# A hybrid encoder layer: fixed instruction orders from the decay terms to the merge, one step of each chain per weight piece

## The chip, the cores and the metric

One Trainium2 chip, of which the kernel uses 1 core. The metric is the device time of one execution in microseconds (us), as the median of several runs; lower is better. An interval is a 95% one.

## The reference

One layer over 272 positions (16 learned meta tokens and 256 inputs) of width 2048, in float32. One projection `u @ w_in` feeds everything; branch A is a bidirectional mLSTM with 4 heads of 256, branch B a differential attention with 8 heads. The change touches branch A's core and B's queries and keys:

```python
u = rmsnorm(h, norm1_g[layer])
proj = u @ w_in[layer]
m_qk, m_v, m_o, m_gates, d_q, d_k, d_v, g_m, g_d = jnp.split(proj, split_at, axis=-1)
...
qk = jax.nn.silu(dwconv_centred(m_qk, conv_w))
q, k = jnp.split(qk, 2, axis=-1)
...
# one direction, per chunk of the scan
dmat = jnp.where(lower, b[..., :, None] - b[..., None, :] + li[..., None, :], -jnp.inf)
s = jnp.einsum('bhtd,bhsd->bhts', q, k) * jnp.exp(dmat - m_t[..., None])
den = jnp.sum(s, axis=-1) + a_t * jnp.einsum('bhd,bhtd->bht', n, q)
h = num / jnp.maximum(jnp.abs(den), jnp.exp(-m_t))[..., None]
...
# both directions
hs = (h_fwd + h_bwd)[:, :, pad:]
hn = (hs - mu) * lax.rsqrt(var + EPS)
...
q = rope_partial(q, cos, sin)
k = rope_partial(k, cos, sin)
```

The kernel writes the scan as whole 258-column maps: per head one table of decays (`FB`) times the scores, in both directions, without chunks.

## The kernel before

**Weights.** All products run as fp32r pairs: an operand is split into `hi`, its rounded copy, and `lo`, the rest, and a product is three matmuls. The weights come in pieces of 512 KB (`pieces`, from the DMA queue on SP), each split by ACT (`hi` cast, line 157) and DVE (`lo` subtract, line 115) into one of four buffers. `weights()` hands out a piece and prepares the one three ahead. A block of `gemm` makes 256 output columns from four pieces, 24 matmuls to a piece, in two of three PSUM tiles `acc`; after its last piece `evac` copies both halves out, so the second half of the next block waits for the first copy of this one.

**Stages.** After an opening that computes Q's first block and the 16 gate columns, `weave(front, back)` interleaves a front, which is a generator of small steps, with blocks of weights: one front step, then one piece. The fronts are `decay_terms` (gates to decay rows `rows` and columns `aT`, lines 479 to 538) over the rest of Q and all K; `heads1` (lines 655 to 667: per head the decay table, scores, their product, and the sums `den`) over V; `heads2` (lines 726 to 747: reciprocal, spread, merge of both directions, output product, norm) over DQ. DK and DV follow with `run`, without a front.

**Where work waits.** Apart from the opening, the order in which an engine takes its instructions is made by a scheduler from the dependences and its own estimates of time; each engine then works strictly in that order. `in_order()` replaces this for what is written inside it: each instruction is tied behind the one written before it on its engine. The opening uses it already. `later` is a list of functions that `gemm` calls (`flush()`) after the next piece's matmuls.

**POOL.** For each head POOL broadcasts a row of `rows` over 128 partitions (line 606), masks six parts of it (line 609), and later adds four parts of the weighed scores (line 164). PSUM has besides `acc` one tile `one` and two tiles `two`; `den` holds one of the latter through `heads1`.

Of the kernel before, what the change touches and what calls it, by code (L numbers as in the profile page):

```python
# [12 lines left out]
AF = mybir.ActivationFunctionType  # L13
# [51 lines left out]
def hybrid_layer(ctx, tc, x, meta, norm1_g, w_in, conv_w, gate_bias, mnorm_g, lq1, lk1, lq2, lk2,  # L65
# [259 lines left out]

    def rsqrt(r, ss, n, work, bias=eps):

        a, t = work
        activation(r, ss, AF.Ln, bias=bias, scale=1.0 / n)
        activation(r, r, AF.Exp, scale=-0.5)  # L330
        V.tensor_scalar(out=a, in0=ss, scalar1=1.0 / n, scalar2=bias, op0=ALU.mult, op1=ALU.add)
        V.scalar_tensor_tensor(out=t, in0=r, scalar=-0.5, in1=r, op0=ALU.mult, op1=ALU.mult)
        mul(t, t, a)
        V.scalar_tensor_tensor(out=r, in0=t, scalar=1.5, in1=r, op0=ALU.add, op1=ALU.mult)
# [113 lines left out]
    def conv_silu(dst, f, r, nt):  # L448
        hi, lo = pair(nt)
        dst.append((hi, lo))  # L450

        def evac(ci, a):
            j = f + ci
            u, c = r1(nt), r1(nt)
            mul(u, a, r)
            S.activation(c, u, AF.Copy, scale=cw(1, j))
            V.scalar_tensor_tensor(out=c[:, 1:nt], in0=u[:, 0:nt - 1], scalar=cw(0, j), in1=c[:, 1:nt],
                                   op0=ALU.mult, op1=ALU.add)
            V.scalar_tensor_tensor(out=c[:, 0:nt - 1], in0=u[:, 1:nt], scalar=cw(2, j), in1=c[:, 0:nt - 1],  # L459
                                   op0=ALU.mult, op1=ALU.add)  # L460
            activation(c, c, AF.Silu)
            split(hi[:, ci, :], lo[:, ci, :], c)
        return evac

    put = conv_silu(qs, 0, rQ, NT)
# [11 lines left out]
    rows = rbp.tile([P, WN], F32, tag="rb", name="rows")  # L477

    def decay_terms():

        pli, plf = two(), two()
        for d in range(2):
            PE.matmul(pli[:, d, :L], sel[0:32, d * P:(d + 1) * P], gsb[0:32], start=True, stop=True)
            PE.matmul(plf[:, d, :L], sel[0:32, (2 + d) * P:(3 + d) * P], gsb[0:32], start=True, stop=True)
        li, lf, e, y, w = (unit([2, L]) for _ in range(5))
        S.copy(lf, plf[:, :, :L])
        S.copy(li, pli[:, :, :L])

        S.activation(e, lf, AF.Abs)
        activation(e, e, AF.Exp, scale=-1.0)  # L490
# [53 lines left out]
        for b in range(1, 4):  # L544
            yield from gemm(w_in, 16, Q0 + 256 * b, 256, us, T0, NT, conv_silu(qs, 2 * b, rQ, NT))

    weave(decay_terms(), chain(queries(), keys()))


    def values(c0, centred):  # L550

        v0 = [vsm.tile([P, 1024], F32R, tag="vsm", name="v0") for _ in range(2)]
        for t in v0:
            G.memset(t.bitcast(F32), 0.0)
        vs = []

        def put(b):
            v = pair(256)
            vs.append(([v0[0][:, 256 * b:256 * b + 256], v[0][:, 0, :], v[0][:, 1, :]],
                       [v0[1][:, 256 * b:256 * b + 256], v[1][:, 0, :], v[1][:, 1, :]]))  # L560
            vT = []

            def turn():
                pv = two()
                for ci in range(2):
                    for s in range(3):
                        s0 = ST[s][0]
                        PE.transpose(pv[:, ci, P * s:P * (s + 1)], vT[ci][:, s0:s0 + P], ident)  # L568
                pvs = pv[:, :, 0:384].rearrange("p c (s x) -> p s c x", s=3)
                if centred:  # L570

                    mu = sm(3)
                    V.tensor_reduce(out=mu, in_=pvs, axis=AX.XY, op=ALU.add)
                    V.tensor_scalar(out=mu, in0=mu, scalar1=-1.0 / 256, scalar2=None, op0=ALU.mult)
                for s in range(3):
                    n = ST[s][1]
                    ps = pvs[0:n, s]
                    hi, lo = (vs[b][i][s][0:n].rearrange("p (c x) -> p c x", c=2) for i in range(2))
                    if centred:
                        S.activation(hi, ps, AF.Identity, bias=mu[0:n, s:s + 1], scale=1.0)  # L580
                        V.scalar_tensor_tensor(out=lo, in0=ps, scalar=mu[0:n, s:s + 1], in1=hi.bitcast(F32),
                                               op0=ALU.add, op1=ALU.subtract)
                    else:
                        split(hi, lo, ps)

            def evac(ci, a):
                t = r1(L)
# [12 lines left out]
    W, den = [], two()  # L600
    PARTS_W = [(F0c, 0, 0, 258), (F1c, 1, 2, 256), (F2c, 2, 130, 128)], [(B2c, 2, 0, 258), (B1c, 1, 0, 130), (B0c, 0, 0, 2)]

    def decays(h):
# [11 lines left out]
        mask(FB[0:16, B0c:B0c + 2], 2, -T0, 1)  # L615
        mask(FB[:, B1c + 2:B1c + 130], P, 0, 1)
        mask(FB[:, B2c + 130:B2c + 258], P, 0, 1)
        for d, parts in enumerate(PARTS_W):
            for at, s, _, n in parts:
                ap = FB[:, at:at + n]  # L620
                activation(ap, ap, AF.Exp, bias=aT[:, d, s, h:h + 1], scale=1.0)

    def scores(h):
        FB = W[h]
        ps, p0 = two(), one()
        sc = [p0[:, 0:NT], ps[:, 0, 0:NT], ps[:, 1, 0:NT]]
        for s, (s0, n) in enumerate(ST):

            product(sc[s], [([t[:, c, s0:s0 + P] for t in ks[h]], [t[:, c, :] for t in qs[h]]) for c in range(2)])
        for parts in PARTS_W:  # L630
            for at, s, q, n in parts:
                r = ST[s][1]
# [8 lines left out]
        add(r[:, 0:130], FB[:, B2c:B2c + 130], FB[:, B1c:B1c + 130], G)  # L641
        add(f[0:16], f[0:16], FB[0:16, F0c:F0c + NT], G)
        add(r[0:16, 0:2], r[0:16, 0:2], FB[0:16, B0c:B0c + 2], G)
        hi, lo = t2([2, NT], F32R), t2([2, NT], F32R)
        split(hi, lo, fs)
        return hi, lo
# [5 lines left out]

    en = unit([2, NT])

    def heads1():
        activation(en, m[:, :, T0:L], AF.Exp, scale=-1.0)
        decays(0)
        yield
        for h in range(4):
            if h < 3:  # L660
                decays(h + 1)
            hl = scores(h)
            yield
            yield
            yield
            sums(h, hl)
            yield

    vm, gen = values(V0, True)
    weave(heads1(), gen)  # L670


    hn = []
# [14 lines left out]
    def merged(h, rc):  # L688
# [7 lines left out]
        add(FB[:, F1c:F1c + P], FB[:, F1c:F1c + P], FB[:, B1c + 2:B1c + 130])  # L696
        V.tensor_copy(FB[:, F1c - 2:F1c], FB[:, B1c:B1c + 2])
        add(FB[:, B2c + 130:B2c + 258], FB[:, B2c + 130:B2c + 258], FB[:, F2c:F2c + P])
        hl = rbs.tile([P, 2, WN], F32R, tag="w", name="hl")
        hi, lo = hl[:, 0, :], hl[:, 1, :]  # L700
        split(hi[:, 0:774], lo[:, 0:774], FB[:, 0:774])
# [2 lines left out]
    def outputs(h, hl):  # L704
        num = two()
        for c in range(2):
            product(num[:, c, 0:NT], [([vm[h][i][s][:, P * c:P * (c + 1)] for i in range(2)],
                                       [t[:, 258 * s:258 * s + 258] for t in hl]) for s in range(3)])
        sq, hi, lo = t2([2, NT]), t2([2, NT], F32R), t2([2, NT], F32R)
# [3 lines left out]
        return num, hi, lo  # L713

    def normed(h, num, hi, lo):
# [3 lines left out]
        rsqrt(r, var, 256, (r1(), r1()))  # L719
        u = unit([2, NT])  # L720
        hn.append(u)
        for c in range(2):
# [1 line left out]
                                   op0=ALU.mult, op1=ALU.mult)  # L724

    def heads2():
        rec = unit([2, NT])
        S.activation(rec, den[:, :, 0:NT], AF.Abs)
        V.tensor_tensor(out=rec, in0=rec, in1=en, op=ALU.max)
        V.reciprocal(rec, rec)  # L730
        rhl = pair(NT)
        split(*rhl, rec)
        yield
        hl = merged(0, spread(0, rhl))
        yield
        yield
        for h in range(4):
            if h < 3:
                rc = spread(h + 1, rhl)
            o = outputs(h, hl)  # L740
            yield
            if h < 3:
                hl = merged(h + 1, rc)
            normed(h, *o)
            yield
            yield
            yield


    shuffle = [i + 8 if i < 8 else i - 8 if i < 16 else i for i in range(32)]  # L750
# [2 lines left out]
    def roped(dst, c0, t0, nt):  # L753
        def put(b):
            u = unit([2, nt])
            hi, lo = pair(nt)
            dst.append((hi, lo))

            def evac(ci, a):
                S.copy(u[:, ci, :], a)  # L760
                if ci == 1:
                    table = lambda i: rope[:, i:i + 1, t0:t0 + nt].to_broadcast([P, 2, nt])
                    sw = unit([2, nt])
                    V.stream_shuffle(sw, u, shuffle)
                    mul(sw, sw, table(1), G)
                    mul(u, u, table(0))
                    add(u, u, sw)
                    split(hi, lo, u)
            return evac

        for b in range(4):
            yield from gemm(w_in, 16, c0 + 256 * b, 256, us, t0, nt, put(b))

    weave(heads2(), roped(dq, DQ0, T0, NT))
    run(roped(dk, DK0, 0, L))
    vd, gen = values(DV0, False)
    run(gen)

# [359 lines left out]
```

## Time and profile before

| | us |
|---|---|
| median of 3 runs (1567.14 to 1570.07) | 1569.33 |
| the profiled execution | 1567.37 |
| its span | 1565.5 |
| PE busy | 1542.6 (99%) |
| DVE busy | 1028.6 (66%) |
| ACT busy | 763.7 (49%) |
| POOL busy | 81.0 (5%) |

PE runs the matmuls, DVE and ACT the elementwise work, POOL is the slow fourth engine, SP issues DMAs. The profile's list of waits gives for each engine what ended its idle times; the timeline gives single instructions with the idle time ahead of them in brackets; the table of windows gives busy time and PE's granted clock (1.00 is full speed) in chosen stretches. Times are from the start of the span.

### The profile page before, as it was taken

The page shows a single profiled execution, that of the slowest core. Times are in us where ns is not written, and L with a number is a line of the kernel's source. Part 1 is how long each engine was busy: PE and PEld are TensorE (multiplying, and loading weights), DVE is VectorE, ACT ScalarE, POOL GpSimd, SP SyncE. Part 2 cuts the span into 40 slices and gives each one's busy share as a digit, 9 for nine tenths or more (in the row PEclk, how much of TensorE's full clock was granted, in tenths as well). Part 3 has the DMA queues.
Part 4 walks back from the last instruction along what each step waited for, and adds up shares of the span by engine and source line. Part 5 has one row for each costly group of instructions (what it writes and reads, how often), then busy time and mean ns, then how long its engine had stood idle before and what let it go on. Part 6 is the DMA issues. An engine that isn't in the chain of part 4 may idle for free.

```text
span 1565.5 us, 28927 instructions
## 1 busy us (share of the span) xinstructions
PE 1542.6 (99%) x11825; PEld 1491.2 (95%) x11825; DVE 1028.6 (66%) x1617; ACT 763.7 (49%) x1147; POOL 81.0 (5%) x120
## 2 busy tenths in 40 slices
PE   8899989999999999999999999999999999999997
PEld 8899989999999999999999999999888999999887
DVE  6786688758886545665666676666444676766554
ACT  5656445444655433554555444444333444545443
POOL 1130113100000000000110000000000000000000
PEclk9999999999999999999999999999999999999999
DMA  8365425654356655555555556555555556655552
GB/s 261 110 202 161 148 83 166 189 166 132 122 175 202 185 179 188 181 180 185 193 169 181 187 185 187 181 183 180 198 190 188 187 177 188 185 181 185 184 195 95
DMA packets 255386, 274.53 MB, mean 175 GB/s; under 512 B 11492, under 2 KB 233317, under 8 KB 255237
## 3 DMA queue, kind: packets, MB, share of 16 engines
q1 hardware_dynamic: 251378, 268.61, 54.1%
q10 hardware_dynamic: 3875, 4.07, 0.8%
q8 instruction: 93, 1.52, 0.4%
q14 instruction: 40, 0.33, 0.1%
HBM read 270.55 MB, written 2.10 MB: 174 GB/s over the span
## 4 chain that ended last, share of the span: by engine, by line
PE 95%; DVE 2%; ACT 1%; issue 1%; POOL 0%; DMA 0%; SPq 0%; DVEq 0%; POOLq 0%; ACTq 0%
PE acc L172 90%; PE two L172 2%; DVE lo L115 1%; PE two L846 1%; PE one L172 0%; PE one L858 0%; PE two L568 0%; POOL t L712 0%; ACT hi L157 0%; DMA r<-in_norm_g_dram 0%; PE two L977 0%; PE two L965 0%; DVE u L730 0%; DVE u L115 0%; POOL t L164 0%
## 5 line engine op out<-in xcount | busy, mean ns | idle before, releaser
L172 PE MATMUL acc<-u,hi 128*128 128x258 f32 (+1 forms) x6592 | 1201.8, 285 | 4.8 <-DVE r L161 4.8
L172 PEld LDWEIGHTS acc<-u,hi 128*128 128x128 f32 x6592 | 1019.0, 190 | 7.1 <-DVE r L161 5.1
L172 PE MATMUL acc<-u,lo 128*128 128x258 f32 (+1 forms) x3296 | 925.3, 284 | 0.8 <-DVE lo L115 0.8
L115 DVE TENSOR_TENSOR lo<-raw,hi 128x1024 fp32r<-128x1024 f32 (+1 forms) x500 | 616.8, 1234 | 422.1 <-ACT hi L157 420.4
L157 ACT CAST hi<-raw 128x1024 fp32r<-128x1024 f32 (+1 forms) x500 | 523.7, 1048 | 648.1 <-PE acc L172 501.5
L172 PEld LDWEIGHTS acc<-u,lo 128*128 128x128 f32 x3296 | 622.3, 190 | 1.9 <-DVE lo L115 1.2
L172 PE MATMUL acc<-hi,u 128*128 128x512 f32 (+1 forms) x704 | 209.6, 381 | 0.0
L172 PEld LDWEIGHTS acc<-hi,u 128*128 128x128 f32 x704 | 130.7, 190 | 26.3
L172 PE MATMUL acc<-lo,u 128*128 128x512 f32 (+1 forms) x352 | 134.9, 383 | 0.0
L172 PEld LDWEIGHTS acc<-lo,u 128*128 128x128 f32 x352 | 66.2, 188 | 13.6
L161 DVE TENSOR_TENSOR r<-acc,r 128x258 f32<-128x258 f32 x88 | 37.3, 424 | 12.2 <-PE acc L172 12.2
L115 DVE TENSOR_TENSOR u<-r,u 128x256 fp32r<-128x256 f32 (+2 forms) x93 | 37.7, 435 | 4.9 <-ACT u L157 4.4
L1025 ACT ACTIVATE r<-r,fcT 128x256 f32<-128x256 f32 x88 | 39.8, 500 | 0.0
L157 ACT CAST u<-r 128x256 fp32r<-128x256 f32 (+2 forms) x93 | 34.4, 404 | 9.7 <-DVE r L161 7.0
L1026 DVE SCALAR_TENSOR_TENSOR r<-r,fcT,r 128x256 f32<-128x256 f32 x88 | 38.5, 479 | 0.0
L1027 DVE SCALAR_TENSOR_TENSOR r<-r,fcT,r 128x255 f32<-128x255 f32 x88 | 38.4, 478 | 0.0
L151 ACT ACTIVATE r<-r 128x256 f32<-128x256 f32 (+2 forms) x77 | 29.5, 412 | 3.5 <-DVE r L459 3.1
L161 DVE TENSOR_TENSOR r<-r,r 128x256 f32<-128x256 f32 (+1 forms) x57 | 22.1, 420 | 0.1
L161 DVE TENSOR_TENSOR r<-acc,u 128x258 f32<-128x258 f32 x32 | 13.5, 422 | 12.9 <-PE acc L172 12.9
L164 DVE TENSOR_TENSOR u<-acc,u 128x512 f32<-128x512 f32 (+1 forms) x18 | 10.6, 626 | 13.9 <-PE acc L172 13.9
L161 DVE TENSOR_TENSOR r<-acc,rB 128x272 f32<-128x272 f32 (+1 forms) x38 | 16.1, 429 | 4.8 <-PE acc L172 4.7
L151 ACT ACTIVATE t<-two,sm 128x272 f32<-128x272 f32 x32 | 15.3, 482 | 5.5 <-DVE sm L802 5.5
(246 smaller groups left out, 754.6 us busy)
## 6 DMA issues: line engine op xcount, KB each, us to landing
raw<-in_w_up_dram SPq DMA_DIRECT2D x176, 512.0 KB, 3.9
raw<-in_w_in_dram SPq DMA_DIRECT2D x175, 512.0 KB, 3.5
raw<-in_w_down_dram SPq DMA_DIRECT2D x88, 512.0 KB, 3.7
raw<-in_w_out_dram SPq DMA_DIRECT2D x32, 512.0 KB, 3.3
raw<-in_w_branch_m_dram SPq DMA_DIRECT2D x16, 512.0 KB, 3.3
raw<-in_w_branch_d_dram SPq DMA_DIRECT2D x16, 512.0 KB, 3.2
t<-in_x_dram ACTq DMA_DIRECT2D x8, 256.0 KB, 3.4
xc<-in_x_dram SPq DMA_DIRECT2D x3, 512.0 KB, 6.3
```

Source lines behind the costliest of these rows:

```text
L115: V.tensor_tensor(out=out, in0=src, in1=hi.bitcast(F32), op=ALU.subtract)
L151: a = S.activation(out, in_, func, **kw)
L157: S.copy(hi, src)
L161: eng.tensor_tensor(out=o, in0=a, in1=b, op=ALU.mult)
L164: eng.tensor_tensor(out=o, in0=a, in1=b, op=ALU.add)
L172: PE.matmul(o, p, q, start=first and i == 0, stop=last and i == len(ops) - 1)
L846: PE.matmul(ps[:, i, 0:L], dq[h // 2][p][o:o + 64, h % 2, 2 + P * qt:2 + P * (qt + 1)], dk[h // 2][q][o:o + 64, h % 2, :], start=(p, q) == ...
L1025: S.activation(z, u[:, 2:NT], AF.Copy, scale=fcT[:, 1, f:f + 1])
L1026: V.scalar_tensor_tensor(out=z, in0=u[:, 1:NT - 1], scalar=fcT[:, 0, f:f + 1], in1=z, op0=ALU.mult, op1=ALU.add)
L1027: V.scalar_tensor_tensor(out=z[:, 0:SEQ - 1], in0=u[:, 3:NT], scalar=fcT[:, 2, f:f + 1], in1=z[:, 0:SEQ - 1], op0=ALU.mult, op1=ALU.add)
```

## The change

All three stages are put inside `in_order()`, and DK's run joins DQ's. Each chain's work is cut in steps of which one comes per piece, by further `yield`s or by `later`: the convolution into taps, SiLU and rest; the rotation into swap, join and low; V's centred parts behind their transposes; the merge, its split, the squares, the variance and the norm of a head into steps of their own. `decay_terms` starts behind three pieces. `broadcast(h)` is split off `decays(h)`: 0 and 1 at the start of `heads1`, 2 and 3 behind the weighing of heads 0 and 1. `sums(h)` comes three pieces behind the weighing, the last ones early in `heads2`. The absolute value of `den` is taken by DVE in place of ACT. PE's matmuls are the same in number and shape.

```diff
+        def taps():
+            for ci, (u, c) in enumerate(uc):
+                S.activation(c, u, AF.Copy, scale=cw(1, f + ci))
...
+            later.append(silu)
+        def silu():
+            for ci, (_, c) in enumerate(uc):
+                activation(c, c, AF.Silu)
+                S.copy(hi[:, ci, :], c)
+            later.append(rest)
+        def rest():
+            for ci, (_, c) in enumerate(uc):
+                low(lo[:, ci, :], c, hi[:, ci, :])
...
     def decay_terms():
+        for _ in range(3):
+            yield
...
-    weave(decay_terms(), chain(queries(), keys()))
+    with in_order():
+        weave(decay_terms(), chain(queries(), keys()))
...
     def heads1():
         activation(en, m[:, :, T0:L], AF.Exp, scale=-1.0)
-        decays(0)
+        broadcast(0)
+        broadcast(1)
         yield
         for h in range(4):
-            if h < 3:
-                decays(h + 1)
-            hl = scores(h)
-            yield
-            yield
-            yield
-            sums(h, hl)
-            yield
+            yield
+            decays(h)
+            yield
+            if h:
+                sums(h - 1, last[-1])
+            sc = scores(h)
+            yield
+            fs = weighed(h, sc)
+            if h < 2:
+                broadcast(h + 2)
+            yield
+            last.append(halved(fs))
...
-    weave(heads1(), gen)
+    with in_order():
+        weave(heads1(), gen)
...
     def heads2():
+        yield
+        sums(3, last[3])
+        yield
         rec = unit([2, NT])
-        S.activation(rec, den[:, :, 0:NT], AF.Abs)
-        V.tensor_tensor(out=rec, in0=rec, in1=en, op=ALU.max)
+        V.scalar_tensor_tensor(out=rec, in0=den[:, :, 0:NT], scalar=-1.0, in1=en, op0=ALU.mult, op1=ALU.max)
+        V.tensor_tensor(out=rec, in0=den[:, :, 0:NT], in1=rec, op=ALU.max)
+        yield
         V.reciprocal(rec, rec)
+        yield
         rhl = pair(NT)
         split(*rhl, rec)
         yield
-        hl = merged(0, spread(0, rhl))
-        yield
+        rc = spread(0, rhl)
+        yield
+        FB = merged(0, rc)
+        yield
+        hl = halves(FB)
         yield
...
-    weave(heads2(), roped(dq, DQ0, T0, NT))
-    run(roped(dk, DK0, 0, L))
+    with in_order():
+        weave(heads2(), chain(roped(dq, DQ0, T0, NT), roped(dk, DK0, 0, L)))
```

What this does to the engines' orders is seen at three places. (In these rows `x2` is two of the same in a row.)

POOL, from the end of the opening through V, before: `ISA` without names is a configuration instruction, `ISA FB<-rows` a broadcast, line 609 a mask, line 164 the adds.

```order
L161 TENSOR_TENSOR u<-u,rB 128x272 x2
L606 ISA
L606 ISA FB<-rows 128x1034 x4
L609 AFFINE_SELECT FB<-FB 16x2
L609 AFFINE_SELECT FB<-FB 128x128 x2
...
L164 ISA
L164 TENSOR_TENSOR t_1715<-FB 128x128
L164 TENSOR_TENSOR t_1715<-FB 128x130
L164 TENSOR_TENSOR t_1715<-t_1715,FB 16x2
L164 TENSOR_TENSOR t_1715<-t_1715,FB 16x258
L164 TENSOR_TENSOR t_1926<-FB 128x128
```

The same place now, from the masks of broadcast 1 (now line 637) on, with the broadcast now at line 634.

```order
L637 AFFINE_SELECT FB<-FB 128x128 x2
L164 ISA
L164 TENSOR_TENSOR t_1804<-FB 128x128
L164 TENSOR_TENSOR t_1804<-FB 128x130
L164 TENSOR_TENSOR t_1804<-t_1804,FB 16x258
L164 TENSOR_TENSOR t_1804<-t_1804,FB 16x2
L634 ISA
L634 ISA FB<-rows 128x1034
L637 AFFINE_SELECT FB<-FB 16x2
...
L164 ISA
L164 TENSOR_TENSOR t_2015<-FB 128x128
```

Broadcasts 2 and 3 have moved behind the adds of heads 0 and 1, and with them come four more configuration instructions; the sums of heads 0 to 2 each have one ahead now.

ACT, from the copy of `rB` on, before (line 456 is the middle tap of the convolution, 151 and 147 an activation, 157 a cast):

```order
L157 CAST hi<-raw 128x1024 x2
L429 COPY rB<-one 128x272
L157 CAST hi<-raw 128x1024
L456 ACTIVATE r_517<-r_516,prmT 128x258
L456 ACTIVATE r_526<-r_525,prmT 128x258
```

The same place now (line 459 is the middle tap, 470 the cast of the convolution's result):

```order
L432 COPY rB<-one 128x272
L491 ACTIVATE r_522<-r_522,gb 32x272
L459 ACTIVATE r_517<-r_516,prmT 128x258
L459 ACTIVATE r_520<-r_519,prmT 128x258
L147 ACT_TABLE_LOAD
L147 ACTIVATE r_517<-r_517 128x258
L470 CAST u<-r_517 128x258
L151 ACTIVATE r_520<-r_520 128x258
L470 CAST u<-r_520 128x258
L157 CAST hi<-raw 128x1024 x2
```

The casts of the next weight pieces stand behind the convolution of Q's first block now, where they were around the copy of `rB`.

PE, at the change from V to DQ, now (line 593 is V's transposes, `two<-t,selr` the sums of the last head):

```order
L172 MATMUL acc<-u,lo 128x258
L593 MATMUL two<-ident,r_2407 128x128 x3
L593 MATMUL two<-ident,r_2409 128x128 x3
L172 MATMUL two<-t_2424,selr 128x258
L172 MATMUL two<-t_2425,selr 128x258
L172 MATMUL two<-t_2424,selr 128x258
L172 MATMUL two<-t_2425,selr 128x258
L172 MATMUL acc<-u,hi 128x258 x2
```

The four products stand together behind DQ's first piece and the transposes; before, the scheduler had put them singly between matmuls of DQ's second piece.

## Rows read from the trace of the kernel before

**Rows 1.** The page, busy time by engine (us, share of the span, instructions).

```profile
PE 1542.6 (99%) x11825; PEld 1491.2 (95%) x11825; DVE 1028.6 (66%) x1617; ACT 763.7 (49%) x1147; POOL 81.0 (5%) x120
```

**Rows 2.** Waits of PE, 45 to 420 us (us in total, times, longest).

```profile
PE acc L172 <- DVE r L161: 4.8, 1, 4.8
PE two L172 <- issue: 2.8, 1, 2.8
PE two L172 <- DVE u L723: 1.0, 1, 1.0
PE acc L172 <- DVE lo L115: 0.8, 2, 0.5
PE one L172 <- POOL t L712: 0.5, 1, 0.5
PE two L172 <- DVE u L115: 0.3, 1, 0.3
```

**Rows 3.** Timeline of PE (start, duration, instruction, idle before).

```profile
46.33 0.41 PE L172 MATMUL acc<-u,hi 128*128 128x258 f32 x2
...
68.67 0.80 PE L172 MATMUL acc<-u,hi 128*128 128x258 f32 x2 [4.85 <-DVE r L161]
```

**Rows 4.** Windows: length, busy PE, PEld, DVE, ACT, POOL, granted clock, DMA.

```profile
68.70:73.13 4.43, 4.43 (x20) 4.43 (x21) 4.43 (x15) 2.63 (x5) 0.00 (x0) 0.50 0.01 4
...
90.00:195.00 105.00, 105.00 (x853) 105.00 (x852) 69.02 (x112) 58.73 (x100) 11.11 (x25) 1.00 0.54 164
205.00:210.00 5.00, 1.95 (x13) 1.78 (x14) 4.31 (x7) 2.01 (x5) 0.49 (x1) 0.98 0.00 0
210.00:220.00 10.00, 10.00 (x74) 10.00 (x73) 10.00 (x25) 5.63 (x7) 0.70 (x1) 0.84 0.34 105
```

**Rows 5.** Timeline of DVE, 62 to 72 us.

```profile
65.07 0.72 DVE L502 SCALAR_TENSOR_TENSOR u<-u 128x544 f32<-128x544 f32 x1
...
68.21 0.40 DVE L161 TENSOR_TENSOR r<-acc,rB 128x258 f32<-128x258 f32 x1
```

**Rows 6.** Timeline of ACT in the opening.

```profile
41.50 0.39 ACT L429 COPY rB<-one 128x272 f32<-128x272 f32 x1
```

**Rows 7.** Groups of ACT by form, 34 to 225 us (busy, mean ns, idle before).

```profile
L157 ACT CAST hi<-raw 128x1024 fp32r<-128x1024 f32 x52 | 54.2, 1047 | 41.0 <-PE acc L172 39.1 <-issue 1.6
...
L142 ACT ACT_TABLE_LOAD x2 | 2.6, 1283 | 0.0
```

**Rows 8.** Groups of DVE by form, 44 to 225 us.

```profile
L115 DVE TENSOR_TENSOR lo<-raw,hi 128x1024 fp32r<-128x1024 f32 x49 | 62.2, 1269 | 24.3 <-ACT hi L157 23.8
```

**Rows 9.** Groups of PE by form, 100 to 125 us.

```profile
L172 PE MATMUL acc<-u,hi 128*128 128x272 f32 x135 | 25.3, 287 | 0.0
L172 PE MATMUL acc<-u,lo 128*128 128x272 f32 x68 | 19.5, 288 | 0.0
```

**Rows 10.** Timeline of DVE at the end of V.

```profile
194.80 1.16 DVE L633 SCALAR_TENSOR_TENSOR FB<-two,FB 128x256 f32<-128x256 f32 x4 [1.77 <-PE two L172]
...
199.02 0.70 DVE L115 TENSOR_TENSOR t<-t,t 128x516 fp32r<-128x516 f32 x1 [1.44 <-ACT t L157]
```

**Rows 11.** Line 606 alone (duration min/median/max in ns, first and last start).

```profile
L606 POOLq MODIFY_POOL_CONFIG  x2: 11/11/11, 43.9 to 44.0; - x2
```

**Rows 12.** Timeline of POOL, 40 to 270 us.

```profile
74.42 6.06 POOL L606 PARTITION_BROADCAST FB<-rows  x4 [30.45 <-PE acc L172]
80.32 12.44 POOL L609 TENSOR_SCALAR_AFFINE_SELECT FB<-FB 16x2 f32<-16x2 f32 x24
...
179.37 0.41 POOL L164 TENSOR_TENSOR t<-FB 128x128 f32<-128x128 f32 x1 [13.23 <-DVE FB L633]
...
181.10 0.18 POOL L164 TENSOR_TENSOR t<-t,FB 16x2 f32<-16x2 f32 x1
```

**Rows 13.** The page, DMA issues (KB each, median us to landing).

```profile
raw<-in_w_in_dram SPq DMA_DIRECT2D x175, 512.0 KB, 3.5
...
xc<-in_x_dram SPq DMA_DIRECT2D x3, 512.0 KB, 6.3
```

More of the change, by code (lines that the diff above doesn't have):

```diff
@@ L326, in rsqrt, with newton @@
     def rsqrt(r, ss, n, work, bias=eps):
-        a, t = work
         activation(r, ss, AF.Ln, bias=bias, scale=1.0 / n)
         activation(r, r, AF.Exp, scale=-0.5)
+        newton(r, ss, n, work, bias)
+    def newton(r, ss, n, work, bias=eps):
+        a, t = work
         V.tensor_scalar(out=a, in0=ss, scalar1=1.0 / n, scalar2=bias, op0=ALU.mult, op1=ALU.add)
@@ L450, in conv_silu @@
         dst.append((hi, lo))
-        def evac(ci, a):
[L453 to L462, printed above, removed]
+        uc = []
+        def taps():
+            for ci, (u, c) in enumerate(uc):
+                S.activation(c, u, AF.Copy, scale=cw(1, f + ci))
+            for ci, (u, c) in enumerate(uc):
+                V.scalar_tensor_tensor(out=c[:, 1:nt], in0=u[:, 0:nt - 1], scalar=cw(0, f + ci), in1=c[:, 1:nt],
+                                       op0=ALU.mult, op1=ALU.add)
+                V.scalar_tensor_tensor(out=c[:, 0:nt - 1], in0=u[:, 1:nt], scalar=cw(2, f + ci), in1=c[:, 0:nt - 1],
+                                       op0=ALU.mult, op1=ALU.add)
+            later.append(silu)
[7 more added lines that the diff above has]
+                low(lo[:, ci, :], c, hi[:, ci, :])
+        def evac(ci, a):
+            uc.append((r1(nt), r1(nt)))
+            mul(uc[ci][0], a, r)
+            if ci == 1:
+                later.append(taps)
         return evac
@@ L569, in turn, with parts @@
                 pvs = pv[:, :, 0:384].rearrange("p c (s x) -> p s c x", s=3)
+                mu = sm(3)
                 if centred:
-                    mu = sm(3)
                     V.tensor_reduce(out=mu, in_=pvs, axis=AX.XY, op=ALU.add)
                     V.tensor_scalar(out=mu, in0=mu, scalar1=-1.0 / 256, scalar2=None, op0=ALU.mult)
+                later.append(lambda: parts(pvs, mu))
+            def parts(pvs, mu):
                 for s in range(3):
@@ L601, in hybrid_layer, with broadcast @@
     PARTS_W = [(F0c, 0, 0, 258), (F1c, 1, 2, 256), (F2c, 2, 130, 128)], [(B2c, 2, 0, 258), (B1c, 1, 0, 130), (B0c, 0, 0, 2)]
-    def decays(h):
+    def broadcast(h):
         FB = rbp.tile([P, WN], F32, tag="rb", name="FB")
@@ L617, in decays @@
         mask(FB[:, B2c + 130:B2c + 258], P, 0, 1)
+    def decays(h):
+        FB = W[h]
         for d, parts in enumerate(PARTS_W):
@@ L623, in scores @@
     def scores(h):
-        FB = W[h]
         ps, p0 = two(), one()
@@ L629, in scores, with weighed @@
             product(sc[s], [([t[:, c, s0:s0 + P] for t in ks[h]], [t[:, c, :] for t in qs[h]]) for c in range(2)])
+        return sc
+    def weighed(h, sc):
+        FB = W[h]
         for parts in PARTS_W:
@@ L643, in scores, with halved @@
         add(r[0:16, 0:2], r[0:16, 0:2], FB[0:16, B0c:B0c + 2], G)
+        return fs
+    def halved(fs):
         hi, lo = t2([2, NT], F32R), t2([2, NT], F32R)
@@ L653, in hybrid_layer @@
     en = unit([2, NT])
+    last = []
     def heads1():
         activation(en, m[:, :, T0:L], AF.Exp, scale=-1.0)
-        decays(0)
+        broadcast(0)
+        broadcast(1)
         yield
         for h in range(4):
-            if h < 3:
-                decays(h + 1)
-            hl = scores(h)
             yield
+            decays(h)
             yield
+            if h:
+                sums(h - 1, last[-1])
+            sc = scores(h)
             yield
-            sums(h, hl)
+            fs = weighed(h, sc)
+            if h < 2:
+                broadcast(h + 2)
             yield
+            last.append(halved(fs))
     vm, gen = values(V0, True)
-    weave(heads1(), gen)
+    with in_order():
+        weave(heads1(), gen)
     hn = []
@@ L698, in merged, with halves @@
         add(FB[:, B2c + 130:B2c + 258], FB[:, B2c + 130:B2c + 258], FB[:, F2c:F2c + P])
+        return FB
+    def halves(FB):
         hl = rbs.tile([P, 2, WN], F32R, tag="w", name="hl")
@@ L708, in outputs, with squared @@
                                        [t[:, 258 * s:258 * s + 258] for t in hl]) for s in range(3)])
+        return num
+    def squared(num):
         sq, hi, lo = t2([2, NT]), t2([2, NT], F32R), t2([2, NT], F32R)
@@ L712, in outputs, with variance @@
         G.tensor_tensor(out=lo, in0=sq, in1=hi.bitcast(F32), op=ALU.subtract)
-        return num, hi, lo
-    def normed(h, num, hi, lo):
+        return hi, lo
+    def variance(hi, lo):
         var = one()[:, 0:NT]
@@ L718, in normed @@
         r = r1()
-        rsqrt(r, var, 256, (r1(), r1()))
+        activation(r, var, AF.Ln, bias=eps, scale=1.0 / 256)
+        activation(r, r, AF.Exp, scale=-0.5)
+        return var, r
+    def normed(h, num, var, r):
+        newton(r, var, 256, (r1(), r1()))
         u = unit([2, NT])
@@ L733, in heads2 @@
         yield
-        hl = merged(0, spread(0, rhl))
+        rc = spread(0, rhl)
         yield
+        FB = merged(0, rc)
+        yield
+        hl = halves(FB)
         yield
         for h in range(4):
+            num = outputs(h, hl)
+            yield
+            hi, lo = squared(num)
             if h < 3:
                 rc = spread(h + 1, rhl)
-            o = outputs(h, hl)
             yield
             if h < 3:
-                hl = merged(h + 1, rc)
-            normed(h, *o)
+                FB = merged(h + 1, rc)
             yield
+            if h < 3:
+                hl = halves(FB)
+            var, r = variance(hi, lo)
             yield
+            normed(h, num, var, r)
             yield
+            if h < 3:
+                yield
     shuffle = [i + 8 if i < 8 else i - 8 if i < 16 else i for i in range(32)]
@@ L757, in put, with swap, join @@
             dst.append((hi, lo))
+            sw = unit([2, nt])
+            table = lambda i: rope[:, i:i + 1, t0:t0 + nt].to_broadcast([P, 2, nt])
+            def swap():
+                V.stream_shuffle(sw, u, shuffle)
+                mul(sw, sw, table(1), G)
+                mul(u, u, table(0))
+                later.append(join)
+            def join():
+                add(u, u, sw)
+                S.copy(hi, u)
+                later.append(lambda: low(lo, u, hi))
             def evac(ci, a):
@@ L761, in evac @@
                 if ci == 1:
[L762 to L768, printed above, removed]
+                    later.append(swap)
             return evac
```

## The prediction

> **What bounds the kernel now.** The page's busy table is read first: PE, the tensor engine, is busy for 1542.6 us, 99% of the span [rows 1], so only PE's idle time and its slow stretches can be won here, and any wait of PE is paid in full. The diff touches the stretch from 45 to 420 us. There the list of waits [rows 2] gives every stop of PE: one of 4.8 us for DVE's copy `r` out of `acc`, one of 2.8 us ahead of a `two` product, and small ones; 10.2 us in all. PE's timeline puts the longest ahead of 68.67 us [rows 3], and the table of windows the second between 205 and 210 [rows 4]. The windows also tell what comes after [rows 4]: PE's granted clock is 0.50, its lower level of 1.2 GHz, for 4.43 us after the first, which is half of that, 2.2 us, lost; its mean is 0.84 over the 10 us from 210 on, 1.6 us lost. So the stretch loses 10.2 + 2.2 + 1.6 = **14.0 us**, and no edit that leaves PE's matmuls alone can win more there. The profiled execution took 1567.4 us, 2.0 below the runs' median of 1569.3; I make the sum against the profiled one and carry the difference over to the median.
>
> **The change, part by part.**
>
> *The first stop (opening, Q and K).* DVE's timeline [rows 5] shows its cause: the decay chain runs in one go from 65.07 us, and the copy out of `acc` for which PE waits comes behind it, at 68.21. The fixed order gives the chain one step per piece, so this queue goes. What is late next? A fixed order also keeps ACT to the written one, and there the weights' `hi` casts now stand behind all of Q block 0's convolution. From the copy of `rB`, which ends at 41.9 [rows 6]: two DVE multiplies (0.7 by the neighbouring 0.4 us forms), then the pair of ACT taps, the table load of 1.28 [rows 7], two SiLU and two casts, each taken as the 0.39 of that copy, one `hi` of 1.05 [rows 7] and one `lo` of 1.27 [rows 8]. The first tap's half microsecond and the DVE taps lie beside the table load, so 41.9 + 0.7 + 0.5 + 1.3 + 1.6 + 1.05 + 1.25 = 48.3 us. PE has by then used up the eight pieces that are prepared before the order begins. PE's matmuls, counted from the start of its block, end the eighth at 46.4 us (the pair at 46.33 is its last) [rows 3], so a stop of 1.9. Counted in the same way down DVE's new queue, the copy out of `acc` behind the next two `lo` is 1.0 late, and the one behind the decay terms' first Exp (a second table load, one `hi` and two `lo` stand ahead of it) 2.0 late. That is 4.9, and one half-clock spell: I take the smaller of the two measured, 1.6. So 6.5 here, where before it was 4.8 + 0.8 + 2.2 = 7.8. The rest of the decay chain is the same instructions and costs PE nothing: it lies under DVE's idle time.
>
> *V and the scores, without POOL.* One block of V is 4 pieces of 24 matmuls of 272 columns. 203 of these ran in 25.0 us of a full PE [rows 9], so a piece is 2.96 us, and one of 258 columns 2.81 by the ratio. With 22 matmuls of 258 columns for the sums and scores (0.117 each, 2.6) and six short transposes a block and one head take **15.0 us**. Over 105 us of this stage DVE was busy for 69.0 and ACT for 58.7 [rows 4], 9.9 and 8.4 of each 15.0, so the new fixed order costs PE nothing by itself.
>
> *The end of V.* The second stop [rows 2] lies behind the last head's sums and DVE's reciprocal. Now the reciprocal is a step of its own with nothing behind it that PE is due for, but sums(3) are put one piece after halved(3). From the weighing of the last head to the end of its `lo` the trace has 194.80 to 199.72, 4.9 us [rows 10]; ahead of it DVE has an `acc` copy and part of a `lo`, 1.4. PE comes to sums(3) after one piece and six transposes, 2.8 + 0.6 = 3.4 us. So PE stops for 6.3 - 3.4 = 2.9, and again 1.6 of half clock: 4.5 remains of what before was 2.8 + 0.3 + 1.6 = 4.7. The later stops of 1.0 and 0.5 in DQ [rows 2] go, since squares, variance and merge have a piece each; the rotation's steps likewise lie under pieces.
>
> *Sum without POOL's switches:* before 14.0, after 6.5 + 4.5 = 11.0, so **-3.0**: 1566.3.
>
> *POOL.* Here the order shows something that the diff does not say. Before, POOL had all four broadcasts in one row, then one untitled instruction, then all sums. Now each broadcast stands between two such instructions: one ahead of it, one ahead of the next head's adds, six in all where there were two. In the trace they are MODIFY_POOL_CONFIG, always in pairs [rows 11]: POOL is configured anew for the broadcast and its masks, and again for the adds. What does such a switch cost, from the record to the first instruction that can run? The two known to the trace were hidden. The record itself is 11 ns [rows 11], and that is the lower bound; the upper one is the 30.4 us from 44.0 to the first broadcast, in which POOL was waiting for its data anyway [rows 12]. Between ends so far apart I assume that each of the two records fetches something from memory before POOL goes on, and go by the nearest row of a fetch, the landing of a 512 KB weight piece, 3.5 us at the median [rows 13]. **S = 7.0 us**, an estimate.
>
> Per head POOL now has two switches, a broadcast of 1.5 and six masks of 0.52 each, 3.1 [rows 12], and four adds from 179.37 to 181.28, 1.9 [rows 12]: 2S + 6.5 us, serially, against 15.0 on PE. At S = 7 that is 20.5: POOL is 5.5 us per head behind. How much is covered? The adds of a head end about 7.0 us after PE's scores (piece 3.0, copies out of `acc` 0.8, weighing 1.3, adds 1.9); PE wants the next `lo` that DVE has queued behind halved(h) three pieces and the transposes later, at 12.3, and the cast, halved `lo` and that `lo` take 2.5 of it, so the adds may end at 9.8. The cover is 2.8 us, once. Broadcasts 0 and 1 lie ahead, and the last head's adds need no new switch, so heads 1 and 2 alone pay: 2 x 5.5 - 2.8 = **8.2** us. PE stops twice for several us, so two half-clock spells of 1.6: 3.2. In all +11.4.
>
> The Trainium skill (GPSIMD Engine Reference, section 2.1 Instruction dispatch) says that the first call into a freshly loaded GpSimd kernel pays about 6 us (5.95 measured), with no instruction visible in the profile. No row here shows such a wait, as both switches are hidden. By it the two heads would cost 2 x 3.4 - 2.8 = 4.0 and 3.2 of clock, and the time would be 1573.5: the same sign, inside the forecast's own range below.
>
> **Sum:** -3.0 + 11.4 = +8.4 us on 1569.3: **1578 us**, 0.5% slower. The chance of it is put below.
>
> **The rivals.**
>
> *A: the switch is short or mostly hidden, S under 4.95.* There 2S + 6.5 - 15.0 is no more than half of the cover for each of the two heads, and POOL keeps up. Then the -3.0 is left: **1566.3**, not slower. For it: an 11 ns record [rows 11]. Against: two records each time, which an engine would hardly need for nothing.
>
> *B: the fixed orders do what they are meant to, and the switch is short too.* My count of late `lo` in the opening hangs on about 2 us of start times, and sums(3) may find its `lo` ready. Then nearly all 14.0 go: **1555**. Against it: in the order the two `hi` do stand behind four convolution steps, and sums(3) stands one piece behind.
>
> *C: the switch is served behind the weights' stream.* Under the opening's load a 512 KB transfer took 6.3 us [rows 13], not 3.5. Then S = 12.6, POOL's head 31.7, and 2 x 16.7 - 2.8 = 30.6, with 3.2 of clock and less 3.0: +30.8, **1600**. Against it: PE's stops would also stop the stream, and the load comes back to the median's row.
>
> **How the numbers follow.** Forecast 0.57, A 0.20, B 0.10, C 0.13. The forecast's own range goes by S from 5.5 to 8.5 and 2 us for the opening: 1570 to 1586. The range over all cases reaches down to A less some 4 us for the opening, 1562, and up to S = 10.7, half way into C, 1593; B and the far half of C are left out, about 0.17. About 0.2%, 3.1 us, is what a measurement of this kernel can tell from no change. B and half of A, with a little of the forecast's lower end, are faster by more: 0.22. The other half of A and 0.08 of the forecast: 0.18. Slower 0.60.
>
> **What would show it.** In the changed kernel's profile POOL's timeline should show a gap of about 7 us, with no releaser that explains it, ahead of each of broadcasts 2 and 3 and of the adds of heads 1 and 2; PE waits in V, for `lo` or through it for `two`, of some 3 and 5 us, each followed by a granted clock of 0.5 for some 4 us; none in V before them. In the opening three stops of 1 to 2 us at about 46, 50 and 62 us in place of the 4.8; one of 3 ahead of the last sums; no 1.0 in DQ. Wrong, if POOL's gaps are below 5 us or no stop of PE follows them, if the opening's stops are gone or over 5 us in all, or if PE waits in DK, where I count nothing.

## The result and the profile after

The changed kernel takes **1580.8 us** (median of 4 runs, 1577.3 to 1582.4) against 1569.2 of the kernel before, so 11.6 us slower by the medians; the ratio on record, from all runs of both, is 1.0079, 95% interval 1.0067 to 1.0092. Forecast were 1578, and slower with a chance of 0.60. The profiled execution is the slowest of the four, 1582.4 us with a span of 1580.3. A second trace of the same kernel (experiment `e0_after_again`) has a span of 1577.0.

The page's busy line [rows 1] and the waits of PE from 45 to 430 us [rows 2], both of the changed kernel:

```profile
PE 1550.2 (98%) x11825; PEld 1496.3 (95%) x11825; DVE 1034.6 (65%) x1618; ACT 766.1 (48%) x1148; POOL 80.8 (5%) x120
```

```profile
PE two L172 <- DVE u L609: 5.3, 2, 2.7
PE acc L172 <- DVE r L161: 3.4, 2, 2.7
PE two L172 <- DVE t L115: 2.9, 3, 2.2
PE acc L172 <- DVE lo L115: 2.1, 3, 1.1
PE two L172 <- ACT t L157: 1.4, 2, 1.0
PE acc L172 <- ACT hi L157: 0.6, 1, 0.6
```

PE waits 15.7 us where it waited 10.2. No line of these names POOL, and POOL is busy as long as before. It has to be looked for further back. The products `two<-t` wait for ACT's cast `t`, the rounded copy of the halved scores, and in ACT's timeline that cast waits for POOL's adds:

```profile
166.85 0.62 ACT L157 CAST t<-t 128x516 fp32r<-128x516 f32 x1 [7.02 <-POOL t L164]
...
187.42 0.62 ACT L157 CAST t<-t 128x516 fp32r<-128x516 f32 x1 [6.01 <-POOL t L164]
```

For head 0 this wait is 1.3 us. The step before is seen in POOL's own timeline in V [rows 12]:

```profile
143.05 0.98 POOL L164 TENSOR_TENSOR t<-FB 128x128 f32<-128x128 f32 x2 [36.45 <-DVE FB L667]
...
152.70 1.35 POOL L634 PARTITION_BROADCAST FB<-rows  x1 [6.82 <-issue]
154.12 3.07 POOL L637 TENSOR_SCALAR_AFFINE_SELECT FB<-FB 16x2 f32<-16x2 f32 x6
165.14 0.83 POOL L164 TENSOR_TENSOR t<-FB 128x128 f32<-128x128 f32 x2 [7.94 <-issue]
...
172.89 1.35 POOL L634 PARTITION_BROADCAST FB<-rows  x1 [6.07 <-issue]
...
185.70 0.83 POOL L164 TENSOR_TENSOR t<-FB 128x128 f32<-128x128 f32 x2 [8.11 <-PE acc L172]
```

Four gaps of 6.1 to 8.1 us stand where the order has configuration instructions between the heads; the long gaps ahead of the first and the last head's adds (36.5 and 11.7 us) are ended by their data, DVE's weighed scores. (The last of the four names PE's `acc`, which the adds don't read; their data, from line 667, were there at 180.4.) That POOL isn't waiting for data in the four is seen in line 164 alone, from 150 to 160 us (ns, first and last start):

```profile
L164 POOLq MODIFY_POOL_CONFIG  x2: 1/1/1, 157.2 to 157.3; - x2
L164 POOLq EVENT_SEMAPHORE  x1: 17/17/17, 158.8 to 158.8; - x1
```

The switch is issued at 157.2, the weighed scores are there at 158.8, and the add starts at 165.14: 7.9 us after the switch, 6.3 after its data. What follows on PE, in the timeline and the table of windows [rows 3, 4]:

```profile
167.53 0.39 PE L172 MATMUL two<-t,selr 128*128 128x258 f32 x1 [1.02 <-ACT t L157]
168.25 0.64 PE L172 MATMUL two<-t,selr 128*128 128x258 f32 x3 [0.34 <-DVE t L115]
172.26 2.40 PE L172 MATMUL two<-u 128*128 128x258 f32 x12 [2.64 <-DVE u L609]
```

```profile
60.00:70.00 10.00, 7.29 (x51) 7.08 (x50) 7.68 (x13) 5.52 (x8) 0.00 (x0) 0.85 0.35 109
...
172.00:180.00 8.00, 7.74 (x50) 7.77 (x51) 4.53 (x9) 3.75 (x8) 4.62 (x7) 0.79 0.44 125
187.00:195.00 8.00, 5.00 (x31) 4.39 (x30) 3.27 (x5) 5.73 (x13) 1.65 (x7) 0.90 0.22 66
195.00:205.00 10.00, 7.93 (x57) 7.50 (x55) 8.12 (x15) 4.70 (x8) 1.69 (x4) 0.91 0.52 159
205.00:215.00 10.00, 9.46 (x66) 9.46 (x67) 8.63 (x9) 3.04 (x5) 0.00 (x0) 0.83 0.34 106
```

A head's sums wait for the halved scores; then the next scores wait for V's parts (line 609), which still read the tile `two` that the scores need, and which DVE and ACT do only behind the halved scores. That is 4.0 us, and the next head repeats it with 3.0. The clock tells the rest: length times what the mean lacks of 1.00 is 1.5, 1.7, 0.8 + 0.9 and 1.7, so 6.6 us in four half-clock spells.

### The profile page after: what moved, and what is told of

Same layout as the page of the kernel before. It is cut to its first block, busy times and chain, and to the rows that moved or that the text cites. A ratio compares the mean times of both kernels' runs of the same rounds, so it can differ in the third digit from the quotient of the medians.

```text
span 1580.3 us, 28904 instructions
## 1 busy us (share of the span) xinstructions
PE 1550.2 (98%) x11825; PEld 1496.3 (95%) x11825; DVE 1034.6 (65%) x1618; ACT 766.1 (48%) x1148; POOL 80.8 (5%) x120
## 4 chain that ended last, share of the span: by engine, by line
PE 94%; DVE 2%; SPq 1%; ACT 1%; issue 1%; DMA 1%; POOL 0%; DVEq 0%; ACTq 0%; POOLq 0%
PE acc L172 89%; PE two L172 2%; DVE lo L115 1%; PE two L927 1%; SPq L301 1%; ACT hi L157 0%; PE one L172 0%; PE one L939 0%; DMA t<-in_lambda_k_dram 0%; PE two L593 0%; DMA raw<-in_w_in_dram 0%; PE two L1046 0%; PE two L1058 0%; SPq L275 0%; SPq L290 0%
## 5 line engine op out<-in xcount | busy, mean ns | idle before, releaser
L161 DVE TENSOR_TENSOR r<-acc,r 128x258 f32<-128x258 f32 x88 | 37.3, 424 | 14.6 <-PE acc L172 14.6
L157 ACT CAST u<-r 128x256 fp32r<-128x256 f32 (+1 forms) x77 | 28.1, 403 | 9.4 <-DVE r L161 7.0
L161 DVE TENSOR_TENSOR r<-r,r 128x256 f32<-128x256 f32 (+1 forms) x57 | 22.1, 421 | 0.2
L172 PE MATMUL two<-u 128*128 128x258 f32 (+1 forms) x96 | 16.3, 329 | 5.3 <-DVE u L609 5.3
L843 ACT CAST u<-u 128x516 fp32r<-128x516 f32 (+1 forms) x8 | 5.1, 636 | 32.3 <-DVE u L164 32.3
```

Source lines behind the costliest of these rows:

```text
L157: S.copy(hi, src)
L161: eng.tensor_tensor(out=o, in0=a, in1=b, op=ALU.mult)
L172: PE.matmul(o, p, q, start=first and i == 0, stop=last and i == len(ops) - 1)
L843: S.copy(hi, u)
```

## The experiments

Every kernel ran beside the kernel before on its own chip; ratios are to that, with 95% intervals. The changed kernel stands at 1.0079 and, measured again, at 1.0066.

**All broadcasts at the start.**

```diff
         broadcast(1)
+        broadcast(2)
+        broadcast(3)
         yield
...
-            if h < 2:
-                broadcast(h + 2)
```

> The change with all four broadcasts at the start of heads1, so that POOL is configured twice and not six times; everything else stays. Theory (POOL's switches make the stops in V): the two pairs of stops in V, 1.0 + 0.3 + 2.6 and 0.3 + 2.7 us, go, and with them two half-clock spells of 1.7 us: 7.0 + 3.4 = 10.4 us less than the changed kernel, near 1570.4 us, and POOL's adds start within 0.5 us of the weighing in every head. Rival (the fixed order itself is too tight: the sums wait for the halved scores and the scores for V's parts, whatever POOL does): the stops stay and the time is that of the changed kernel, 1580.8 us.

1568.68 us, ratio 1.0006 (0.9997 to 1.0015): 0.60 to 0.73% less than the changed kernel, 9.4 to 11.5 us. POOL's timeline of this kernel:

```profile
141.59 0.99 POOL L164 TENSOR_TENSOR t<-FB 128x128 f32<-128x128 f32 x2 [28.73 <-DVE FB L667]
...
156.84 1.00 POOL L164 TENSOR_TENSOR t<-FB 128x128 f32<-128x128 f32 x2 [12.41 <-DVE FB L667]
...
172.16 0.94 POOL L164 TENSOR_TENSOR t<-FB 128x128 f32<-128x128 f32 x2 [12.47 <-DVE FB L667]
```

The adds now come 15.3 us apart, each released by its data; in the changed kernel they were 22.1 and 20.6 us apart. V's stops are gone, and the theory holds. This is also the change without its switches between the heads: 0.8 us more than the kernel before by the medians, where the prediction's sum had 3.0 less.

**One switch pair in place of two.**

```diff
         broadcast(1)
+        broadcast(2)
         yield
...
-            if h < 2:
-                broadcast(h + 2)
+            if h == 1:
+                broadcast(3)
```

> The change with broadcasts 0, 1 and 2 at the start and broadcast 3 alone behind the weighing of head 1: POOL is configured four times, one switch pair stands between two heads' adds. Theory (each such pair costs 2S + 6.5 - 15.0 with S of 6 to 8 us, less a cover of 2.8 us once, and one half-clock spell): between the kernel with all broadcasts at the start (no pair, 1568.7 us) and the changed kernel (two pairs): one group of stops of 3 to 4 us in V and a spell of 1.7 us, so 1573.5 us. Rival (only the position of the broadcast counts, and head 3 has time enough): as with all at the start, 1568.7 us.

1574.99 us, ratio 1.0046 (1.0034 to 1.0058), about half way between none and two. Its trace has one group of stops in V, 0.5 + 0.35 + 2.66, behind that pair. So the cost goes with the number of pairs; that a late broadcast without a switch makes no stop in V is seen in the next kernel, which leaves broadcasts 2 and 3 where they are.

**The adds on DVE.**

```diff
-        add(f[:, 130:258], FB[:, F1c + P:F1c + 2 * P], FB[:, F2c:F2c + P], G)
+        add(f[:, 130:258], FB[:, F1c + P:F1c + 2 * P], FB[:, F2c:F2c + P])
...
```

(the other three adds in the same way)

> The change with the four adds of a head on DVE in place of POOL; the broadcasts stay two heads ahead, each at its place, and POOL needs its broadcast configuration alone. Theory (switches): as without them, near 1570.4 us, less or more by 1 us, since DVE takes four adds of 0.3 to 0.4 us per head into its idle time. Rival (the late broadcasts 2 and 3 themselves hold up the decay products, or the fixed order is too tight): V's stops stay and the time is 1580.8 us or, with DVE's load, above.

1563.12 us, ratio 0.9967 (0.9954 to 0.9979): the switches' cost goes by this way too, and 5.6 us more than with all broadcasts at the start. The waits of PE, 45 to 430 us:

```profile
PE acc L172 <- DVE r L161: 3.4, 2, 2.7
PE acc L172 <- DVE lo L115: 1.8, 2, 1.1
PE two L172 <- DVE t L115: 1.0, 1, 1.0
PE acc L172 <- ACT hi L157: 0.6, 1, 0.6
PE two L172 <- ACT t L157: 0.3, 1, 0.3
```

The stop at the last sums is 1.3 in place of 2.6, probably because DVE's adds end sooner than POOL's, and the clock stays at 1.00 from 180 to 200 us. And in this trace the clock also stays at 1.00 behind the opening's 2.7 us stop, which in the changed kernel it didn't; of that part the cause is open, and it isn't so in every run: two of the five have a mean clock of 0.999, the other three 0.996 to 0.997 and 1563.1 to 1564.0 us. Another 2.8 us of the gain lie behind all that was changed (see the sum, below).

**The adds on DVE in the kernel before** (the same four lines, in the kernel before).

> The kernel before, with the four adds of a head on DVE and nothing else. It has no switch between the heads, so this tells what the adds' engine is worth by itself. Theory (the gain in the changed kernel is that of the switches, not of DVE's faster adds): within 2 us of the kernel before, 1568 us. Rival (the adds on DVE are the gain, whatever the switches do): 4 us less or more.

1571.16 us, ratio 1.0019 (1.0011 to 1.0028): 3 us slower, so neither expectation holds to its number, but the adds' engine by itself is no gain. The control isn't a clean one: the order here is the scheduler's, and its new one stops PE for 5.4 us ahead of the first spread, where it was 2.8.

**The changed kernel again.**

> The changed kernel itself once more, so that it stands on the same chip as the others of this call. Theory: between 1578 and 1581 us; V again stops PE for 6 to 8 us in two places behind POOL's second and third switch pair, each gap on POOL between 5.5 and 8.5 us. If the share of the opening (1.9 us at 28 us in the profiled run, where nothing was changed) is chance, it has another size here. Rival: the stop at 28 us comes with the change's schedule and is there again in the same size.

1578.34 us, ratio 1.0066 (1.0054 to 1.0078). V's stops are there again (1.05 + 0.34 + 2.65 and 2.63). The 1.9 us ahead of 28 us, in the first trace followed by a mean clock of 0.90 up to 45 us, is not: it was chance (kernels with the same opening have 0.15 to 1.9 there). The half-clock spell itself is in the second trace too, at 8 us; at PE's 300th matmul the first trace is 2.2 us behind, most of the 3.3 us between the two.

**The first stage without a fixed order.**

```diff
-    with in_order():
-        weave(decay_terms(), chain(queries(), keys()))
+    weave(decay_terms(), chain(queries(), keys()))
```

> The change without the fixed order around the decay terms with Q and K; V and DQ keep theirs. Theory (in this stage the fixed order takes the 4.8 us stop away and brings 4.7 us of others): within 2 us of the changed kernel, and the stops at 46 to 53 us go while one of 2 to 5 us stands somewhere in Q or K. Rival (the fixed order here is what costs): 4 to 6 us less than the changed kernel, 1575 us.

1572.00 us, ratio 1.0023 (1.0013 to 1.0034). The theory falls, the rival holds: 6.3 us less than the changed kernel on the same chip. From 45 to 130 us PE has no stop at all in this trace, and it starts its 1000th matmul, early in V, at 134.8 us where the changed kernel on that chip has 142.0; so the gain is the opening's. With the steps cut as the change cuts them, the scheduler no longer makes the 4.8 us queue of [rows 5]; it is the fixing that brings the new ones.

**A better fixed order for the opening.**

```diff
             if ci == 1:
-                later.append(taps)
+                behind_pieces(2 if f == 0 else 0, taps)
...
         V.tensor_tensor(out=e, in0=e, in1=w, op=ALU.subtract)
+        yield
         activation(y, y, AF.Ln)
```

(`behind_pieces(n, step)` appends a step to `later` n pieces later.)

> The change with the convolution of Q's first block two pieces later, so that the weight casts stand ahead of it on ACT, and with the decay terms' Ln and second Exp one piece later. Theory (the opening's stops of 0.6, 0.75, 0.7 and 2.7 us are weight casts and copies out of acc that queue behind those): all 4.7 us go and the half-clock spell of 1.6 us with them, 6.3 us less, 1574.5 us. Rival (they come back further on, as the steps that moved queue ahead of later casts): between 1578 and 1581 us.

1571.50 us, ratio 1.0025 (1.0015 to 1.0035): 0.4 to 0.5% less, 6.4 to 8.5 us. Of the four stops one of 0.57 is left, but the gate products now come 1.4 us before their gates, with a clock of 0.89 over 45 to 60 us. In its trace V's first group of stops is also down to 0.38 from 4.0. At its 1000th matmul PE is only 3.4 us ahead of the changed kernel's second trace, where the theory had 6.3, so the larger part of the gain is V's.

**The last sums two pieces later.**

```diff
         yield
+        yield
+        yield
         sums(3, last[3])
```

> The change with the last head's sums, and all of heads2 behind them, two pieces later. Theory (PE stops there for 2.6 us because the halved scores of the last head are not ready one piece behind): the stop and its half-clock spell of 1.7 us go, 4.3 us less than the changed kernel, 1576.5 us; V's stops stay. Rival (the stop only moves, to the reciprocal's chain or to a tile that den holds longer): 1580.8 us.

1575.37 us, ratio 1.0050 (1.0038 to 1.0063). The stop at the sums is gone, but another stands ahead of the first spread in PE's timeline:

```profile
217.32 0.36 PE L172 MATMUL two<-u 128*128 128x258 f32 x1 [1.67 <-issue]
218.01 0.63 PE L172 MATMUL two<-u 128*128 128x258 f32 x3 [0.33 <-DVE u L115]
```

2.0 us in place of 2.6, and the clock falls behind it too (0.93 over 215 to 240 us). The rival holds for most of it: the stop moved. The 2.5 to 4.5 us gained are partly V's second stop, 1.66 for 2.65 here.

**All edits together.** The adds on DVE, both edits of the opening with the gate products one piece later, the sums two pieces later, and:

```diff
     def heads2():
...
+        for i, v in enumerate((lq1, lq2, lk1, lk2)):
+            nc.scalar.dma_start(out=lv[:, i, :], in_=v.to_broadcast([P, 64]))
         rec = unit([2, NT])
```

> All together: adds on DVE, the last sums two pieces later, Q block 0's convolution two pieces later, Ln a piece later, the gate products a piece later, and the four small loads of the lambda vectors moved from behind DV into the merge. Theory (each stop has its own cause and they add up): from the kernel with the adds on DVE, 1563.1 us, another 4.7 us of the opening's stops with up to 1.7 of clock, 1.3 at the end of V and 1.1 in DK go, 8 us: 1555 us. Rival (a stop that goes comes back in the next queue): 1560 to 1563 us.

1564.64 us, ratio 0.9982 (0.9974 to 0.9991). The opening is down to two stops of 0.7 without a fall of the clock, V has none, but one line of PE's timeline takes it back:

```profile
205.80 0.55 PE L172 MATMUL two<-u 128*128 128x258 f32 x1 [4.82 <-issue]
```

The four loads are issued by ACT, a weight cast comes late behind them, and DVE, which waits 2.7 us for it, starts the reciprocal at 199.2 only. The rival's number is missed by 2 us, its mechanism is what happened.

**First stage free, adds on DVE.** The edits of those two kernels.

> The change without the fixed order around the decay terms with Q and K, and with the four adds of a head on DVE. Theory (two costs that add: the fixed order of the opening, some 6 to 7 us, and POOL's switches with what the last head's adds hold up, some 15): 1563.1 us of the kernel with the adds on DVE less 6 us, near 1557 us; no stop of PE between 45 and 185 us. Rival (both draw on the same slack of DVE, and the scheduler's order meets DVE's adds): 1562 us or above.

1558.46 us, ratio 0.9939 (0.9926 to 0.9953): the two costs add. All waits of PE, 45 to 430 us:

```profile
PE acc L172 <- DVE lo L115: 1.1, 1, 1.1
PE two L172 <- DVE t L115: 1.0, 1, 1.0
PE two L172 <- ACT t L157: 0.3, 1, 0.3
```

**The same, with two pieces more for the last sums and the spread.**

```diff
         yield
+        yield
         sums(3, last[3])
...
         split(*rhl, rec)
         yield
+        yield
         rc = spread(0, rhl)
```

> As the kernel of the line before (first stage free, adds on DVE), with the last head's sums one piece later and one piece more between the reciprocal's split and the first spread. Theory (the sums need one piece more, and the two pieces of the earlier run only moved the stop because the spread then met its split too early): the last stop of 1.3 us goes and none takes its place before the output products; 1.3 us less than that kernel, about 1556 us. Rival (as in the run with the sums two pieces later, a stop of 2 to 5 us ahead of the first spread): 1558 to 1562 us.

**1554.84 us**, ratio 0.9917 (0.9903 to 0.9930), faster than both kernels: 13.0 us under the kernel before, which lost 14.0 in this stretch. Against the kernel of the run before it gains 3.6 us, but not by what the theory named: its stop of 1.3 us is gone, and one of 2.2 stands further on. Of the 4.9 us between the two traces 1.2 come before PE's 3300th matmul, DK's wait of 1.1 among them, and 3.7 after it, where nothing was edited (see the sum, below). The one stop left is ahead of the first output product, and the clock doesn't fall behind it:

```profile
PE two L172 <- DVE hl L115: 2.2, 1, 2.2
```

## Why the prediction was right, point by point

**POOL's switches: right, in place and size.** The estimate was S = 7.0; measured are 6.8 and 6.1 ahead of the broadcasts, 7.9 and 8.1 ahead of the adds, a mean of 7.2. The period of POOL was forecast at 20.5 and came out at 22.1 and 20.6. Undone in two unlike ways (the broadcasts back, the adds away) and halved in a third, it changed the time as it should. The assumption under the 7.0, two fetches as long as a weight piece's landing, is not shown by that; only its sum is, and that it came out so near is luck. The 5.95 us of the Trainium skill (GPSIMD Engine Reference, section 2.1 Instruction dispatch) is near the smallest gap measured here and 2 us below the larger two.

**The cover: mis-sized.** The step "the cover is 2.8 us, once" is off. POOL's adds came 22.1 + 20.6 - 2 x 15.3 = 12.1 us late in all, the term had 11.0; PE lost 7.0, the term had 8.2; so 5.1 us were covered. The two errors partly cancel. I let PE's stop come at the `lo` of the piece three on; the trace has it at the sums, which need the halved scores, and at the next scores, which need the tile that V's parts still read. (The 105 us of [rows 4] that I read as V hold part of K too. V alone, from 135 to 195 us, has DVE busy for 37.3 and ACT for 31.2 of 60 us, so that they have room stands.)

**The half-clock spells: right in sum.** Forecast were four of 1.6, 6.4 us; measured 6.6.

**The opening: right in sum, wrong as an account of the change.** Forecast were 4.9 us of stops at 46, 50 and 62; the trace has 4.7, as 0.6, 0.75 and 0.7 between 49 and 53 us and 2.7 ahead of 67.3. The terms were 1.9 (measured 1.3 in two stops), 1.0 (0.7) and 2.0 (2.7), so the sum is right by errors that cancel. In the second trace PE starts its 1000th matmul 1.1 us earlier than in the kernel before (142.0 against 143.1 us), where the sum says 1.3. But the sum set stop against stop, and did not ask what the cut steps are worth without the fixed order. The run with the first stage free is 8.3 us ahead of the kernel before at that matmul (134.8), of which the fixing gives back 7.2.

**The last sums: right,** 2.9 forecast, 2.6 measured, with the spell. Removing it alone proved harder than the text makes it look: two pieces more made the spread wait.

**DK: wrong,** and by the prediction's own list of signs. I counted nothing there; PE waits 1.4 us in all, in the first trace, and 1.1 to 1.3 in most. The scheduler puts the lambda vectors' loads and sums, which stand behind the fixed stretch and are tied to nothing, into DK's last pieces. DVE sits there for 3.5 us until one load lands, and PE's wait for a `lo` follows:

```profile
302.21 0.29 DVE L161 TENSOR_TENSOR t<-t 128x128 f32<-128x128 f32 x1 [3.47 <-DMA t<-in_lambda_k_dram]
```

```profile
313.06 0.39 PE L172 MATMUL acc<-u,lo 128*128 128x272 f32 x1 [1.09 <-DVE lo L115]
```

In every trace in which DVE waits 3.0 us or more for that load, PE waits 1.1 to 1.4 here; with the last sums later DVE waits only 0.6 to 0.7 for it, and PE not at all.

**The sum.** +8.4 us forecast, +11.6 measured, +10.0 the second time. In the stretch that the sum covers it is right: forecast were 11.0 + 11.4 = 22.4 us of stops and slow clock, and from 45 to 430 us the first trace has 15.7 + 6.6 = 22.3; V's term came out 1.0 smaller than forecast, and DK's 1.4 make up for it. At PE's 3300th matmul the second trace is 8.2 us behind the kernel before, the first 11.6, the 2.2 of the chance stop among them.

What the sum had at nothing is the part after that. From the 3300th matmul to the end both traces of the changed kernel take 1136.8 us, and the one of the kernel before 1133.6. The matmuls stand in the same order there, PE never waits, and the clock falls only at the very end, in all kernels alike; the matmuls themselves come a little slower. In a window of about the same work the kernel before (first line) gets four more done than the changed one (second):

```profile
750.00:900.00 150.00, 150.00 (x1255) 149.95 (x1255) 97.58 (x132) 77.52 (x117) 8.90 (x12) 1.00 0.57 181
```

```profile
750.00:900.00 150.00, 150.00 (x1251) 149.94 (x1250) 97.53 (x129) 77.25 (x119) 11.08 (x15) 1.00 0.57 182
```

These 3.2 us are not chance between executions, as 1136.8 is measured again in the kernels with all broadcasts at the start, with one late, and with the late sums. Over all traces the part lies between 1133.4 and 1137.1 us. So it is a matter of the program, but no edit was aimed at it and its cause is open. It explains why the kernel with all broadcasts at the start, 1.8 us ahead of the kernel before at the 3300th matmul, ends no faster. The forecast's 1578 falls 2.8 us short of 1580.8 mainly by this term.

## What to carry to other kernels

Read the order for instructions that nobody wrote: a kind of operation placed between two others can bring a change of the engine's configuration at each end, and an engine that is busy 5% of the time can still set the pace of a stage. Count an engine's period with such switches in it, against the period of the engine it feeds. When a change both cuts a chain into steps and fixes an order, try the cut alone: in the first stage here it was worth 6 us more without the fixing. And compare the part that no edit touched by counting matmuls, before a gain or a loss is put down to an edit.

## What the runs showed of the hardware

A switch of POOL's configuration cost 5.8 to 8.1 us until the next instruction in all six traces that have them between the heads, with two records of 1 ns as its only sign; those ahead of adds are the longer ones (6.9 to 8.1 against 5.8 to 6.8).

The same stop of 2.7 us at 65 to 67 us was followed by the lower clock in four traces (mean of 0.83 to 0.87 from 60 to 70 us, and of 0.89 from 60 to 75 us in each) and not in two (1.00): the all-broadcasts kernel and the adds-on-DVE kernel have the same order up to there, and lie on either side:

```profile
60.00:70.00 10.00, 7.31 (x51) 7.10 (x51) 8.14 (x16) 6.22 (x8) 0.00 (x0) 0.87 0.46 126
```

```profile
60.00:70.00 10.00, 7.31 (x61) 7.10 (x60) 8.14 (x16) 6.18 (x8) 0.00 (x0) 1.00 0.46 121
```

Both have PE busy for 7.31 us of the 10, once with 51 matmuls and once with 61. So the same stop cost its own time alone or 1.7 us more (15 us at a mean of 0.89).
